# First feed-forward's gated result in separate tiles of high and low parts, and weights placed 64 bytes beyond the stream mod 256

## The chip, the cores and the metric

The kernel runs on one core of a Trainium2 chip. The metric is device time in microseconds of one execution. A profiled execution gives the trace from which the tables and rows below come; times between single matmuls are read from that.

## The reference

A decoder layer on 272 tokens (16 learned meta tokens ahead of 256) of width 2048: feed-forward, a mixer of differential attention beside a short gated convolution, and a second feed-forward. What bears on the change:

```python
def swiglu_ffn(h, w_gu, w_down):
    gate, up = jnp.split(h @ w_gu, 2, axis=-1)
    return (jax.nn.silu(gate) * up) @ w_down

h = rms_norm(s, norm_ffn1[layer])
s = s + 0.5 * swiglu_ffn(h, ffn1_w_gu[layer], ffn1_w_down[layer])
h = rms_norm(s, norm_mix[layer])
q, k, v, b_gate, c_gate, u = jnp.split(h @ w_in[layer], splits, axis=-1)
...
v = c_gate * u          # short convolution over time, then b_gate * y
```

Everything is float32; the feed-forward's inner width is 5632.

## The kernel before

**Numbers in two parts.** Every matmul operand is split into a high part (a copy as fp32r) and a low part (value minus high part). A product is three matmuls: weights high by activations high, weights high by activations low, weights low by activations high (lines 329 to 331 in `linear`). ScalarE casts the weights from the load buffer `st` into `wh` (line 313), VectorE subtracts into `wl` (line 318).

**A linear.** `linear` computes four 128-wide column groups at once, each in a PSUM bank, over all chunks of 128 contraction rows. Per chunk it issues 4 x 3 matmuls of 128x128 weights by n columns of activations: n = 272 for gate, up, down, k and v, and n = 258 for c and u, which start at token 14 (`n0 = NMETA - 2`). For n up to 256 the high and low parts go through in one matmul of 2n columns. Weights of two chunks share a buffer of `wh` and one of `wl` (three buffers each, from `wpool`); a load (SyncE's queue, 1 MB) brings four chunks into one of four buffers.

**Stages.** The first feed-forward runs in two halves of 6 and 5 groups of 512 inner columns. In each half, `gate_up` runs for each group a linear for gate (`pg`) and one for up (`pu`) over 16 chunks of `h1`, and puts the gated product into `m`; then four down linears (`pd`) run over the half's 24 or 20 chunks of `m`, and add to the stream `s`. After it come k, q, b, v, with attention steps between matmuls, then c and u, the gates and branch projections (`g`, `z`), `w_out` (`o`), and the second feed-forward, which is written with other functions and uses `linear` no more.

**Where operands lie.** A word is 4 bytes. An `Act` tile holds two chunks, each with its high and its low part, one after the other. For `h1` and `h2` a part is 320 words long (1280 bytes) and its 272 tokens begin at word 48, so every part is read from 192 bytes mod 256 of the tile's start. For `m` a part is 272 words (1088 bytes = 4 x 256 + 64), so the four parts of a tile begin at 0 (high, even chunk), 64 (low, even), 128 (high, odd) and 192 (low, odd) mod 256. Weights of a column group begin at a multiple of 512 bytes in `wh` and `wl`. All buffers of `act`, `big`, `wh` and `wl` have sizes that are multiples of 256 bytes, and in the built program all of them start at the same residue mod 256.

**Order.** The order on each engine follows the order of the code, with evictions and small steps put in by chunk number (`EVICT_AT`, `side_at`, `later_at`); a tile's buffer is free when its last reader is done.

Of the kernel before, what the change touches and what calls it, by code (L numbers as in the profile page):

```python
# [9 lines left out]
F32 = mybir.dt.float32  # L10
F32R = mybir.dt.float32r
# [4 lines left out]
P = 128  # L16
D = 2048
SEQ = 256
NMETA = 16
# [3 lines left out]
GC = 4  # L23
GW = GC * P
W2 = D // 2
NH = 8
HD = 64
# [29 lines left out]
def decoder_layer(ctx: ExitStack, tc: tile.TileContext, t, out):  # L57
    nc = tc.nc

    const = ctx.enter_context(tc.tile_pool(name="const", bufs=1))  # L60
    wpool = ctx.enter_context(tc.tile_pool(name="w", bufs=W_BUFS))
    apool = ctx.enter_context(tc.tile_pool(name="a", bufs=N_ACT))
    aux = ctx.enter_context(tc.tile_pool(name="aux", bufs=N_AUX))
    tmp = ctx.enter_context(tc.tile_pool(name="tmp", bufs=2))
    psum = ctx.enter_context(tc.tile_pool(name="ps", bufs=8, space=bass.MemoryType.PSUM))

    def bank(name):
        return psum.tile([P, 512], F32, tag="acc", name=name)

    def wide(shape, name):  # L70
        return tmp.tile(shape, F32, tag="wide", bufs=4, name=name)
# [37 lines left out]
    vrows = const.tile([NV, P], F32, name="vrows")  # L109
    G_MIX, G_FFN2, G_CONV, G_SUB = 0, DC, 2 * DC, NV - 1  # L110

    lamv = const.tile([P, 4, HD], F32, name="lamv")

    def load_vectors():
        for g0, src in ((G_MIX, t["norm_mix"][0]), (G_FFN2, t["norm_ffn2"][0])):
# [11 lines left out]
        out=mask[:, T - P :],  # L127
        in_=mask[:, T - P :],
# [41 lines left out]
    class Act:  # L170


        def __init__(self, name, chunks, width, wide_slots=(), piece=None):
            self.width, self.lead = width, 0 if piece is None else piece - width
            self.tiles = []
            for g in range(chunks // 2):
                if g in wide_slots:
                    w = piece or width
                    raw = apool.tile([P, 4 * PIECE], F32R, tag="big", bufs=N_BIG, name=f"{name}{g}")
                    self.tiles.append(raw[:, : 4 * w].rearrange("p (c l w) -> p c l w", c=2, l=2))  # L180
                else:
                    self.tiles.append(apool.tile([P, 2, 2, width], F32R, tag="act", name=f"{name}{g}"))
# [3 lines left out]

        def part(self, c, lo, t0, t1):
            return self.tiles[c // 2][:, c % 2, lo, self.lead + t0 : self.lead + t1]

    def split(act, g, src):  # L190

        for k in range(2):
            tl, f = act.tiles[2 * g + k], src[:, 2 * k : 2 * k + 2, :]
            nc.scalar.copy(out=tl[:, :, 0, :], in_=f)
            nc.vector.tensor_sub(tl[:, :, 1, :], f, tl[:, :, 0, :].bitcast(F32))
# [73 lines left out]
    def drain():  # L269
        while ahead:  # L270
            ahead.pop(0)[0]()

    def linear(act, chunks, w, k0, c0, t0, t1, name, evict, before=None, side_at=(5, 9, 13), after=None, later_at=LATER_AT):

        n = t1 - t0
        kb = KB
        nl = LB * kb
        starts = list(range(0, len(chunks), kb))  # L280
        if before is not None:
            starts.insert(1, 1)
        acc = [bank(f"{name}_{j}") for j in range(GC)]
        ready = {}
        for b, b1 in zip(starts, starts[1:] + [len(chunks)]):
            blk = chunks[b:b1]
            r0 = (k0 + blk[0]) * P
            wh = wpool.tile([P, kb, GW], F32R, tag="wh", name="wh")
            wl = wpool.tile([P, kb, GW], F32R, tag="wl", name="wl")
            m = len(blk)  # L290
            if before is not None or b % nl == 0:
                st = wpool.tile([P, LB * kb, GW], F32, tag="st", bufs=ST_BUFS, name="st")
                ml = m if before is not None else min(nl, len(chunks) - b)
                with ExitStack() as order:
                    for ins in x_load:
                        order.enter_context(tc.issue_after(ins))
                    x_load.clear()
                    last_load[:] = [
                        nc.sync.dma_start(
                            out=st[:, :ml, :],  # L300
                            in_=w[r0 : r0 + ml * P, c0 : c0 + GW].rearrange("(c p) f -> p c f", p=P),
                        ).ins
                    ]
            sw = st[:, :m, :] if before is not None else st[:, b % nl : b % nl + m, :]
            with ExitStack() as order:
                if before is not None and b == 0:
                    with tc.issue_after(nc.scalar.copy(out=wh[:, :m, :], in_=sw).ins):
                        ready[0] = before(blk)
                if before is not None:
                    for ins in ready.pop(b):  # L310
                        order.enter_context(tc.issue_after(ins))
                if before is None or b:
                    nc.scalar.copy(out=wh[:, :m, :], in_=sw)  # L313
                if before is None and b:
                    for ins in ahead_of_split:
                        order.enter_context(tc.issue_after(ins))
                    ahead_of_split.clear()
                nc.vector.tensor_sub(wl[:, :m, :], sw, wh[:, :m, :].bitcast(F32))  # L318
            if before is not None and b1 < len(chunks):
                ready[b1] = before(chunks[b1 : starts[starts.index(b1) + 1] if b1 < starts[-1] else None])  # L320
            drain()
            for i, c in enumerate(blk):
                first, last = b + i == 0, b + i == len(chunks) - 1
                for j in range(GC):
                    a, f = acc[j][:, :n], slice(j * P, (j + 1) * P)
                    if 2 * n <= 512:
                        nc.tensor.matmul(acc[j][:, : 2 * n], wh[:, i, f], act.both(c, t0, t1), start=first, stop=False)  # L327
                    else:
                        nc.tensor.matmul(a, wh[:, i, f], act.part(c, 0, t0, t1), start=first, stop=False)  # L329
                        nc.tensor.matmul(a, wh[:, i, f], act.part(c, 1, t0, t1), start=False, stop=False)  # L330
                    nc.tensor.matmul(a, wl[:, i, f], act.part(c, 0, t0, t1), start=False, stop=last)  # L331
                if b + i == EVICT_AT:
                    flush()
                if b + i in later_at and later:
                    later.pop(0)()
                if b + i in side_at and side:
                    side.pop(0)()
                if after is not None:
                    after(b + i)
        flush()  # L340
        pending.append(lambda: evict(acc))

    def flush():
        while pending:
            pending.pop(0)()
# [92 lines left out]
    def gate_up(h, half, w_gu, norm, n0, before=None):  # L438

        n = T - n0  # L440
        m = Act("m", len(half) * GC, n)
        for gi, g in enumerate(half):
            sg = wide([P, GC, T], "sg")

            def gate(pg, sg=sg):
                rstd = norm.rstd[:, n0:]
                for j in range(GC):
                    gt = tmp.tile([P, T], F32, tag="gt", name="gt")
                    nc.vector.tensor_mul(gt[:, :n], pg[j][:, :n], rstd)
                    nc.scalar.activation(gt[:, :n], gt[:, :n], AF.Silu)  # L450
                    nc.vector.tensor_mul(sg[:, j, :n], gt[:, :n], rstd)

            def up(pu, sg=sg, gi=gi):
                for j in range(GC):
                    nc.vector.tensor_mul(sg[:, j, :n], pu[j][:, :n], sg[:, j, :n])
                split(m, gi, sg[:, :, :n])

            linear(h, list(range(DC)), w_gu, 0, g * GW, 0, n, "pg", gate, before=before)
            before = None
            linear(h, list(range(DC)), w_gu, 0, F + g * GW, 0, n, "pu", up)  # L460
        return m
# [274 lines left out]
    for half in halves:  # L736
        m = gate_up(h1, half, t["ffn1_w_gu"][0], norm1, 0, before1 if half is halves[0] else None)
# [370 lines left out]
    for half in thirds:  # L1108
        m = Act("m", len(half) * GC, SEQ, range(4))
# [3 lines left out]
        if final:  # L1113
            for q in range(2):
                nc.gpsimd.dma_start(
                    out=gfin[q],
                    in_=t["norm_final"][q * W2 : (q + 1) * W2].rearrange("(o d) -> o d", o=1).to_broadcast([P, W2]),
                )
        ma = Mixed(m, 0, True)
        for u in range(2):  # L1120
# [23 lines left out]
            chunks = list(range(len(half) * GC))  # L1144
# [41 lines left out]
```

## Time and profile before

| | |
|---|---|
| median of 3 runs | 2161.79 us (2161.72 to 2163.14) |
| profiled execution, its own time | 2161.81 us |
| its span, first to last instruction | 2160.0 us |
| TensorE, busy share of the span | 99% |
| VectorE, ScalarE, GpSimd | 73%, 51%, 4% |
| granted TensorE clock, mean | 0.999 |
| DMA engines in the first 700 us | about half busy |

A row of a group gives line, engine, operation, output <- inputs, shape and count, then busy time, mean ns of one, and the idle time before them with what ended it. Matmuls overlap, and their ends are modelled, so their durations add up to more than the time they fill; the time from start to start is what they cost. A row of the windows view gives a stretch of the span, its length, busy time and count of the chosen instructions on each engine, the granted clock, the DMA engines' share and GB/s. PEld is the load of weights into the array, PE the matmul itself.

### The profile page before, as it was taken

What the parts mean: (1) busy time and instruction counts of PE and PEld (TensorE: products, weight loads), DVE (VectorE), ACT (ScalarE), POOL (GpSimd) and SP (SyncE); (2) the same over time, 40 slices, a digit from 0 to 9 for tenths busy, and PEclk for the clock granted to TensorE, in tenths of its full rate; (3) what the DMA queues carried; (4) which work ended last, traced back from release to release, by engine and by line L of the source; (5) the groups of instructions that cost most, each with busy time, mean ns of one, the idle gap of its engine ahead of it and who ended that gap; (6) DMA issues with size and microseconds to landing.
All of it is one profiled execution on the core that took longest, in us unless ns stands there. A gap on an engine that the chain in (4) does not pass through costs nothing.

```text
span 2160.0 us, 33235 instructions
## 1 busy us (share of the span) xinstructions
PE 2147.3 (99%) x13349; PEld 1943.6 (90%) x13349; DVE 1566.5 (73%) x2054; ACT 1091.2 (51%) x1379; POOL 82.8 (4%) x93
## 2 busy tenths in 40 slices
PE   9999999999999999999999999999999999999998
PEld 9999999999999998899998888888888888888886
DVE  8555554445555567866887778678999899988997
ACT  6443343334433444545445555456665566655664
POOL 0000000000000000000000000001100111012100
PEclk9999999999999999999999999999999999999999
DMA  7555555555555555544456556557886989679954
GB/s 256 176 178 180 181 181 174 175 179 181 176 176 176 176 176 191 180 158 136 156 187 203 194 197 222 193 189 237 273 259 198 289 283 281 226 224 312 280 198 156
DMA packets 205216, 440.76 MB, mean 204 GB/s; under 512 B 10557, under 2 KB 11270, under 8 KB 205062
## 3 DMA queue, kind: packets, MB, share of 16 engines
q1 hardware_dynamic: 188118, 398.13, 53.9%
q0 software_dynamic: 16480, 39.85, 8.3%
q8 instruction: 104, 1.70, 0.3%
q10 hardware_dynamic: 464, 0.66, 0.1%
q14 instruction: 50, 0.41, 0.1%
HBM read 431.26 MB, written 2.10 MB: 201 GB/s over the span
## 4 chain that ended last, share of the span: by engine, by line
PE 97%; DMA 1%; DVE 1%; ACT 0%; issue 0%; POOL 0%; SPq 0%; DVEq 0%; ACTq 0%
PE pg L522 6%; PE pg L524 6%; PE pg L523 6%; PE pd L331 4%; PE pd L329 4%; PE pd L330 4%; PE pu L329 4%; PE pu L331 4%; PE pu L330 4%; PE pg L331 4%; PE pg L329 4%; PE pg L330 4%; PE o L327 3%; PE pd L524 3%; PE pd L523 3%; PE pd L522 3%
## 5 line engine op out<-in xcount | busy, mean ns | idle before, releaser
L318 DVE TENSOR_TENSOR wl<-st,wh 128x1024 fp32r<-128x1024 f32 (+1 forms) x361 | 439.9, 1220 | 399.5 <-ACT wh L313 399.1
L313 ACT CAST wh<-st 128x1024 fp32r<-128x1024 f32 (+1 forms) x360 | 376.6, 1047 | 529.8 <-PE pu L330 151.1
L432 DVE TENSOR_TENSOR wl<-st,wh 128x1024 fp32r<-128x1024 f32 (+1 forms) x392 | 437.2, 1122 | 68.6 <-ACT wh L431 66.7
L431 ACT CAST wh<-st 128x1024 fp32r<-128x1024 f32 (+1 forms) x392 | 371.6, 973 | 216.2 <-PE pdx L523 45.1
L431 ACT CAST wh<-t 128x1024 fp32r<-128x1024 f32 x142 | 148.2, 1052 | 206.2 <-DVE t L562 135.3
L432 DVE TENSOR_TENSOR wl<-t,wh 128x1024 fp32r<-128x1024 f32 x142 | 172.3, 1222 | 57.6 <-ACT wh L431 52.7
L329 PE MATMUL pd<-m,wh 128*128 128x272 f32 x704 | 203.0, 288 | 0.0
L331 PE MATMUL pd<-m,wl 128*128 128x272 f32 x704 | 203.0, 288 | 0.0
L330 PE MATMUL pd<-m,wh 128*128 128x272 f32 x704 | 202.4, 288 | 0.0
L329 PE MATMUL pu<-h,wh 128*128 128x272 f32 x704 | 201.9, 287 | 0.0
L331 PE MATMUL pu<-h,wl 128*128 128x272 f32 x704 | 201.7, 287 | 0.0
L330 PE MATMUL pu<-h,wh 128*128 128x272 f32 x704 | 201.7, 287 | 0.0
L329 PE MATMUL pg<-h,wh 128*128 128x272 f32 x704 | 201.6, 287 | 0.0
L330 PE MATMUL pg<-h,wh 128*128 128x272 f32 x704 | 201.2, 287 | 0.1
L331 PE MATMUL pg<-h,wl 128*128 128x272 f32 x704 | 199.6, 287 | 0.1
L524 PE MATMUL pg<-wl,h 128*128 128x512 f32 x399 | 156.2, 391 | 0.0
L523 PE MATMUL pg<-wh,h 128*128 128x512 f32 x399 | 156.2, 391 | 0.0
L522 PE MATMUL pg<-wh,h 128*128 128x512 f32 x399 | 155.5, 390 | 0.0
L330 PEld LDWEIGHTS pg<-h,wh 128*128 128x128 f32 x704 | 132.6, 188 | 0.4 <-DVE h L202 0.4
L329 PEld LDWEIGHTS pg<-h,wh 128*128 128x128 f32 x704 | 132.6, 188 | 0.4 <-ACT h L201 0.2
L330 PEld LDWEIGHTS pd<-m,wh 128*128 128x128 f32 x704 | 132.7, 189 | 0.0
L330 PEld LDWEIGHTS pu<-h,wh 128*128 128x128 f32 x704 | 132.6, 188 | 0.0
(369 smaller groups left out, 4847.7 us busy)
## 6 DMA issues: line engine op xcount, KB each, us to landing
st<-in_ffn_w_gu_dram SPq DMA_DIRECT2D x183, 512.0 KB, 6.1
st<-in_ffn_w_down_dram SPq DMA_DIRECT2D x88, 1024.0 KB, 5.1
st<-in_ffn_w_gu_dram SPq DMA_DIRECT2D x84, 1024.0 KB, 4.9
st<-in_w_in_dram SPq DMA_DIRECT2D x48, 1024.0 KB, 5.2
st<-in_w_gate_dram SPq DMA_DIRECT2D x64, 512.0 KB, 4.3
t<-in_ffn_w_gu_dram POOLq DMA_DIRECT2D x64, 512.0 KB, 7.3
st<-in_w_branch_dram SPq DMA_DIRECT2D x32, 512.0 KB, 4.9
st<-in_w_out_dram SPq DMA_DIRECT2D x16, 1024.0 KB, 5.0
```

The costliest lines, as they stand in the source:

```text
L313: nc.scalar.copy(out=wh[:, :m, :], in_=sw)
L318: nc.vector.tensor_sub(wl[:, :m, :], sw, wh[:, :m, :].bitcast(F32))
L327: nc.tensor.matmul(acc[j][:, : 2 * n], wh[:, i, f], act.both(c, t0, t1), start=first, stop=False)
L329: nc.tensor.matmul(a, wh[:, i, f], act.part(c, 0, t0, t1), start=first, stop=False)
L330: nc.tensor.matmul(a, wh[:, i, f], act.part(c, 1, t0, t1), start=False, stop=False)
L331: nc.tensor.matmul(a, wl[:, i, f], act.part(c, 0, t0, t1), start=False, stop=last)
L431: part_last[:] = [nc.scalar.copy(out=wh, in_=src).ins]
L432: part_last.append(nc.vector.tensor_sub(wl, src, wh.bitcast(F32)).ins)
L522: nc.tensor.matmul(ps[k], hi, wh, start=first, stop=False)
L523: nc.tensor.matmul(ps[k], lo, wh, start=False, stop=False)
L524: nc.tensor.matmul(ps[k], hi, wl, start=False, stop=left[k] == 0)
```

## The change

`m` of the first feed-forward becomes an `Apart`: for each group of four chunks one tile with the high parts and one with the low parts. A part is still 1088 bytes, so chunk c of either tile begins at 64 x (c mod 4) mod 256. For these linears the weights of the two chunks are put into a wider buffer, with a start and a step that put those of chunk c at 64 x (c mod 4 + 1) mod 256. For the other linears the weights start `t0` words into their buffer: 0 for all but c and u, 14 (56 bytes) for those, whose stream starts 14 words later too. Buffers of `wh` and `wl` thus grow from 4096 to 4352 bytes; to make room, `lamv` (1024 bytes, used once for the attention's lambda) takes a buffer of the tag `sc` in place of its own.

```diff
-    lamv = const.tile([P, 4, HD], F32, name="lamv")
+    lamv = tmp.tile([P, 4, HD], F32, tag="sc", name="lamv")
...
+    class Apart:
+        step = GW + NMETA
+
+        def __init__(self, name, chunks, width):
+            self.width = width
+            self.tiles = [
+                [apool.tile([P, GC, width], F32R, tag="act", name=f"{name}{lo}{g}") for lo in "hl"]
+                for g in range(chunks // GC)
+            ]
+
+        def part(self, c, lo, t0, t1):
+            return self.tiles[c // GC][lo][:, c % GC, t0:t1]
+
+        def weights(self, raw, c):
+            f = c % GC * NMETA
+            return raw[:, f : f + 2 * self.step].rearrange("p (c f) -> p c f", c=2)[:, :, NMETA:]
+
+        def split(self, g, src):
+            hi, lo = self.tiles[g]
+            for k in range(2):
+                cs = slice(2 * k, 2 * k + 2)
+                nc.scalar.copy(out=hi[:, cs, :], in_=src[:, cs, :])
+                nc.vector.tensor_sub(lo[:, cs, :], src[:, cs, :], hi[:, cs, :].bitcast(F32))
...
-            wh = wpool.tile([P, kb, GW], F32R, tag="wh", name="wh")
-            wl = wpool.tile([P, kb, GW], F32R, tag="wl", name="wl")
+            if isinstance(act, Apart):
+                wh, wl = (
+                    act.weights(wpool.tile([P, 2 * act.step + 2 * NMETA], F32R, tag=nm, name=nm), blk[0])
+                    for nm in ("wh", "wl")
+                )
+            else:
+                wh, wl = (
+                    wpool.tile([P, t0 + kb * GW], F32R, tag=nm, name=nm)[:, t0:].rearrange("p (c f) -> p c f", c=kb)
+                    for nm in ("wh", "wl")
+                )
...
-        m = Act("m", len(half) * GC, n)
+        m = Apart("m", len(half) * GC, n)
...
-                split(m, gi, sg[:, :, :n])
+                m.split(gi, sg[:, :, :n])
```

On TensorE, at the start of the first half's down linears, chunk 0 and column groups 0 and 1; before:

```order
L329 MATMUL pd_3316<-m_132,wh 128x272
L330 MATMUL pd_3316<-m_132,wh 128x272
L331 MATMUL pd_3316<-m_132,wl 128x272
L329 MATMUL pd_3317<-m_132,wh 128x272
L330 MATMUL pd_3317<-m_132,wh 128x272
L331 MATMUL pd_3317<-m_132,wl 128x272
```

and now:

```order
L363 MATMUL pd_3316<-mh_132,wh 128x272
L364 MATMUL pd_3316<-ml_133,wh 128x272
L365 MATMUL pd_3316<-mh_132,wl 128x272
L363 MATMUL pd_3317<-mh_132,wh 128x272
L364 MATMUL pd_3317<-ml_133,wh 128x272
L365 MATMUL pd_3317<-mh_132,wl 128x272
```

The order is the same; the low part comes from another tile. On VectorE, around the same place (the last eviction of up, then the first down linear's weights), before:

```order
L318 TENSOR_TENSOR wl<-st,wh 128x1024
L195 TENSOR_TENSOR m_142<-sg,m_142 128x2x272
L195 TENSOR_TENSOR m_143<-sg,m_143 128x2x272
L318 TENSOR_TENSOR wl<-st,wh 128x1024 x11
L747 SCALAR_TENSOR_TENSOR s_112<-pd_3316,s_112 128x272
```

and now:

```order
L352 TENSOR_TENSOR wl<-st,wh 128x2x512
L214 TENSOR_TENSOR ml_143<-sg,mh_142 128x544 x2
L352 TENSOR_TENSOR wl<-st,wh 128x2x512 x11
L781 SCALAR_TENSOR_TENSOR s_112<-pd_3316,s_112 128x272
```

Again nothing has moved. The weights' low parts are written as two runs of 512 with a gap, the low parts of `m` as one run of 544. On all five engines every instruction stands where it stood.

## The prediction

> **What bounds the kernel now.** I read the page first: the span, the busy shares and the chain of work that ended last.
>
> ```profile
> span 2160.0 us, 33235 instructions
> PE 2147.3 (99%) x13349; PEld 1943.6 (90%) x13349; DVE 1566.5 (73%) x2054; ACT 1091.2 (51%) x1379; POOL 82.8 (4%) x93
> PE 97%; DMA 1%; DVE 1%; ACT 0%; issue 0%; POOL 0%; SPq 0%; DVEq 0%; ACTq 0%
> ```
>
> TensorE sets the end: 97% of the chain is matmuls. Next the list of waits, on TensorE alone; the columns are total us, times, longest.
>
> ```profile
> PE pd L362 <- DVE wl L432: 1.7, 2, 1.2
> PE warm L82 <- DVE ones L76: 1.1, 1, 1.1
> PE pt L686 <- DMA xin<-in_x_dram: 0.3, 1, 0.3
> PE pd L360 <- ACT wh L431: 0.2, 1, 0.2
> PE c L331 <- DVE wl L318: 0.2, 1, 0.2
> ```
>
> All its waits together are 3.5 us, and none is in a down linear of the first feed-forward. So nothing can be gained there but by matmuls that follow each other faster. How fast they do is not in their durations, which the page's groups give (busy us, mean ns):
>
> ```profile
> L329 PE MATMUL pd<-m,wh 128*128 128x272 f32 x704 | 203.0, 288 | 0.0
> L329 PE MATMUL pu<-h,wh 128*128 128x272 f32 x704 | 201.9, 287 | 0.0
> ```
>
> These overlap (1152 of them at 288 ns would take 332 us, and a window below shows them in 145). What counts is the time from one start to the next, and the windows give that, since each of the following is filled by one kind of matmul. The columns are from:to and length, then TensorE's busy time and count, granted clock, DMA share, GB/s. First four linears of gate and up (tile pu, and tile pg for the last of them), then the down linears of both halves (tile pd).
>
> ```profile
> 83.80:107.48 23.68, 23.68 (x192) 1.00 0.53 178
> 131.16:154.84 23.68, 23.68 (x192) 1.00 0.52 178
> 465.24:488.92 23.68, 23.68 (x192) 1.00 0.51 178
> 441.56:465.24 23.68, 23.68 (x192) 1.00 0.52 179
> ...
> 296.92:441.56 144.64, 144.64 (x1152) 1.00 0.52 175
> 678.36:799.28 120.92, 120.79 (x960) 1.00 0.51 175
> ```
>
> Gate and up: 23.68 / 192 = 123.33 ns a matmul, the same in each of the four. Down: 144.64 / 1152 = 125.56 ns, 2.22 ns more, with the same shape (128x128 weights, 272 columns), the same order of three products, the same clock and the same DMA load. The second down window holds another matmul in its middle:
>
> ```profile
> 687.27 0.29 PE L331 MATMUL pd<-m,wl 128*128 128x272 f32 x1
> 687.49 0.27 PE L150 MATMUL vp<-ident,vrows 57*128 57x57 f32 x1
> 687.68 0.39 PE L329 MATMUL pd<-m,wh 128*128 128x272 f32 x1
> ```
>
> That hole is 0.41 us long where 0.125 would do, so 0.28 us of the 120.92 is not the down linear's: (120.92 - 0.28) / 960 = 125.67 ns. Both halves agree.
>
> What differs is where the operands lie. The timeline shows that they are read together:
>
> ```profile
> 320.02 0.29 PE L330 MATMUL pd<-m,wh 128*128 128x272 f32 x1
> 320.03 0.19 PEld L331 LDWEIGHTS pd<-m,wl 128*128 128x128 f32 x1
> 320.15 0.29 PE L331 MATMUL pd<-m,wl 128*128 128x272 f32 x1
> 320.15 0.19 PEld L329 LDWEIGHTS pd<-m,wh 128*128 128x128 f32 x1
> ```
>
> The load of the next weights starts within 0.01 us of the matmul that streams its 272 columns. For gate, up, k and v the tile width of 320 and the lead of 48 words put the stream at 192 bytes mod 256 of its tile, the weights at 0, so the weights lie 64 beyond it. In the down linears a part is 1088 bytes = 4 x 256 + 64: the four parts of a tile of m stand at 0, 64, 128 and 192, and the weights at 0. Weights thus lie 0, 192, 128 or 64 beyond; 64 only for the low part of odd chunks, one matmul in six.
>
> **The change part by part.** It removes no instruction and adds none. On all five engines the program has the same instructions in the same order, DMAs and their queues too; only addresses, tile names and the folding of some shapes differ. So there is no new wait by order, and the terms are rates.
>
> *Down linears.* With the tiles apart, chunk c of the high or the low tile stands at 64 c mod 256, and the weights, moved by 64 (c + 1), are 64 beyond in all 2112 matmuls. If the distance is what makes 125.6 of 123.33, the first half saves 144.64 - 1152 x 0.12333 = 2.56 us and the second 120.64 - 960 x 0.12333 = 2.24 us: 4.8 us. This price is seen: in the four linears above, of two kinds and from both halves, which read other buffers. Bounds: 0, if the distance isn't the cause, and 4.8, since no 272-column matmul here goes faster than gate and up. I take 4.8.
>
> [...]
>
> *c and u.* They stream from word 14, 56 bytes on, so the stream is at 248 mod 256 of its tile; the weights were at 0, 8 beyond, and are now at 56, 64 beyond. Undisturbed stretches of 258 columns (tile c, tile u), and one of 512 (tile g):
>
> ```profile
> 996.32:1002.04 5.72, 5.72 (x48) 1.00 0.48 174
> 1079.80:1085.52 5.72, 5.72 (x48) 1.00 0.54 186
> ...
> 1195.58:1202.38 6.80, 6.80 (x30) 1.00 0.47 162
> ```
>
> That is 5.72 / 48 = 119.2 ns. From 512 columns (6.80 / 30 = 226.7) to 272 (123.33) a column is worth 0.43 ns, so 258 columns at gate's rate would take 123.33 - 14 x 0.43 = 117.3 ns. There are 768 such matmuls (2 groups, c and u, 16 chunks, 4 x 3): at most 1.9 x 768 = 1.4 us. What the trace does not show is the 64 bytes at a start that is no multiple of 32 bytes; the weights' own reads get such a start now too. Lower bound: the largest excess over gate's rate seen here, 2.3 ns on each, a loss of 1.8 us. The cause is the same as in the down linears, so I lean to the upper end and take 1.0 us.
>
> *What has to keep pace.* In the first half's down linears (windows, all engines: TensorE, weight loads, VectorE, ScalarE, GpSimd; then VectorE's and ScalarE's groups in that window), and in c and u:
>
> ```profile
> 296.90:441.50 144.60, 144.60 (x1154) 144.60 (x1153) 65.66 (x67) 51.53 (x50) 0.00 (x0) 1.00 0.52 175
> 996.30:1104.40 108.10, 107.78 (x892) 104.10 (x891) 82.41 (x164) 53.42 (x108) 0.00 (x0) 1.00 0.46 156
> ...
> L318 DVE TENSOR_TENSOR wl<-st,wh 128x1024 fp32r<-128x1024 f32 x48 | 58.8, 1225 | 78.9 <-ACT wh L313 78.9
> L313 ACT CAST wh<-st 128x1024 fp32r<-128x1024 f32 x48 | 50.4, 1051 | 93.1 <-PE pd L330 85.3 <-DVE s L747 5.8 <-PE pu L330 1.9
> ```
>
> Weights of two chunks need 1.05 us of ScalarE and 1.23 of VectorE, and TensorE takes 24 x 0.123 = 2.96 us for them, with three buffers each. VectorE is idle 78.9 us waiting for the cast, 1.6 us per split. The split now writes two runs of 512 with a gap. No row has that form; from -0.1 to +0.3 us an instruction covers the spread of the forms shown (1.05 to 1.23 for 1024 elements), and all of it is hidden here at the cost of nothing. With no cover it would be 88 splits x 0.3 = 26 us, but for that they would have to become 1.6 us longer. Four casts and subtractions per group of m keep their count, and write whole runs. In c and u VectorE is busy 82 of 108 us; the one wait there is 0.2 us, and I take 0.1 us off the gain for it. The DMA moves 175 GB/s there and 178 under gate's rate, so it follows.
>
> **Sum.** The profiled execution took 2161.81 us, 1.81 beyond its span, and the median of the runs is 2161.79, the same. 4.8 + 1.0 - 0.1 = 5.7 us off: 2161.8 - 5.7 = 2156.1 us. What a measurement tells from no change is about 0.2%, 4.3 us.
>
> **The rivals.** *Distance is not the cause*: stream and weight load leave each other alone, and the down linears are slower for another reason. Then both terms are 0, and the time is 2161.8 us. [...] For it: the 512-column rows of g have distance 0 and still stand at 226.7 in a steady beat. Against: w_out's linear, also at distance 0, which alternates 512 and 256 columns (tile o):
>
> ```profile
> 1371.75:1393.04 21.29, 21.29 (x120) 1.00 0.43 149
> 1428.12:1450.40 22.28, 22.28 (x128) 1.00 0.52 178
> ```
>
> It takes 174 to 177 ns a matmul, where 226.7 and 123.33 - 16 x 0.43 = 116.4 would give a mean of 171.6. And the down linears have no row that sets them apart but the addresses.
>
> *Only part of it.* Gate's stream always starts at one place mod 256, the new down stream at four. If the place counts as well as the distance, one chunk in four gets the gain: 4.8 / 4 = 1.2 us, and c and u nothing: 2160.6 us. Against it: 1088 bytes pass through all residues anyway, whatever the start.
>
> *Slower: the weight buffers' spacing.* A buffer of wh or wl grows from 4096 to 4352 bytes, so the weights of every linear shift against their stream by multiples of 256. If a period above 256 counts, the 4224 matmuls of gate and up and the 768 of k and v could fall to the down linears' old rate: 4992 x 2.2 ns = 11.0 us, 2156.1 + 11.0 = 2167.1 us; it loses from 5.7 / 4992 = 1.1 ns each. Against it: h's tiles are 5120 bytes apart and its parts 1280, so the distances above 256 differ from chunk to chunk already, and the rows of 23.68 do not move.
>
> *It doesn't do what it says*: ruled out as far as addresses go. All act, wh and wl tiles start at one residue mod 256 in the built program, and its 2112 and 768 matmuls all have the 64.
>
> **How the numbers follow.** Forecast (down at gate's rate, c and u somewhere between their bounds): 0.76, from 2161.8 - 4.8 - 1.4 = 2155.6 to 2161.8 - 4.8 + 1.8 = 2158.8. No effect 0.12, a part 0.06, slower 0.06. The range, 2154.3 to 2160.8, takes in the forecast with about 1.3 us of spread between executions (the runs lie 1.4 apart) and the partial case, and leaves out no effect and slower, 0.18. Faster by over 4.3 us, under 2157.5: the forecast unless c and u lose more than 0.5 us, 0.68. Within: the rest of the forecast, no effect, a part, 0.26. Slower: 0.06.
>
> **What would show it.** The windows of pd: 1152 matmuls in about 142.1 us and 960 in about 118.7 (with the hole of 0.28), in the place of 144.64 and 120.92; windows of gate and up again at 23.68. A stretch of 48 matmuls of c or u in 5.63 to 5.68 us; over 5.72 says that the unaligned start costs. VectorE's splits stay under 1.6 us and TensorE's list of waits without a row of pd L331's kind in the first feed-forward. The prediction is wrong if pd stays near 125.5 ns, or if a linear of pg or pu leaves 23.68.

## The result: 3.2 us less, and the profile after

| | before | after |
|---|---|---|
| median of 20 runs each | 2162.14 us (2161.67 to 2166.18) | 2158.93 us (2158.32 to 2161.79) |
| ratio of the times, 95% interval | | 0.9985 (0.9978 to 0.9992) |
| profiled execution, its own time | 2161.81 us | 2158.63 us |

The interval leaves out 1, so the change is a gain, but of 0.15%: less than the 0.2% that the prediction counted as the bound of "no change". The forecast was 5.7 us; 3.2 came. The outcome that the prediction held most likely, faster by over 4.3 us (0.68), did not come. The head of the page of the changed kernel, with the chain's share by engine:

```profile
span 2156.9 us, 33235 instructions
PE 2143.5 (99%) x13349; PEld 1940.6 (90%) x13349; DVE 1566.8 (73%) x2054; ACT 1091.5 (51%) x1379; POOL 82.8 (4%) x93
PE 97%; DMA 1%; DVE 1%; ACT 0%; issue 0%; POOL 0%; SPq 0%; DVEq 0%; ACTq 0%
```

The same instructions, the same bound: TensorE is 3.8 us less busy, the other engines as before. TensorE's waits (total us, times, longest):

```profile
PE pd L396 <- DVE wl L466: 1.7, 2, 1.2
PE warm L82 <- DVE ones L76: 1.1, 1, 1.1
PE pg L363 <- ACT h L227: 0.9, 1, 0.9
...
PE pd L394 <- ACT wh L465: 0.3, 1, 0.3
PE c L365 <- DVE wl L352: 0.2, 1, 0.2
```

No wait has come into a down linear of the first feed-forward (L363 to L365 with pd). The one for h, 0.9 us, is new and lies in the first gate linear, which ends 0.13 us earlier all the same (36.11 us for 36.24). So the difference must be in how closely matmuls follow each other, and the windows of the changed kernel show where (from:to, length, TensorE's busy time and count, clock, DMA share, GB/s): the two halves' down linears (tile pd), two linears of up (pu), a stretch of c and one of u, and the whole stage from the start of c to the end of u.

```profile
296.80:439.68 142.88, 142.88 (x1152) 1.00 0.54 177
676.48:795.97 119.49, 119.36 (x960) 1.00 0.54 177
...
83.68:107.36 23.68, 23.68 (x192) 1.00 0.52 178
463.36:487.04 23.68, 23.68 (x192) 1.00 0.51 178
...
993.00:998.77 5.77, 5.77 (x48) 1.00 0.47 175
...
1076.81:1082.57 5.76, 5.76 (x48) 1.00 0.55 185
...
993.00:1101.59 108.59, 108.38 (x893) 1.00 0.47 155
```

and that last stage in the kernel before:

```profile
996.32:1104.48 108.16, 107.83 (x893) 1.00 0.46 156
```

The down linears gained 144.64 - 142.88 = 1.76 us and 120.92 - 119.49 = 1.43 us, 3.19 together: 142.88 / 1152 = 124.03 ns a matmul in place of 125.56, where 123.33 was expected. Gate and up did not move. c and u, expected to gain 1.0 us, lost: 5.77 / 48 = 120.2 ns in place of 119.2, and their stage is 108.59 - 108.16 = 0.43 us longer. 3.19 - 0.43 = 2.76 of the 3.18 us between the two profiled executions; the rest, 0.4, is in stages whose distances the change leaves alone (0.3 of it in that of g and z), and such amounts come and go between executions (below).

Where in a chunk the down linears lose the rest is seen from the starts of the 12 matmuls (four column groups by three products) of a chunk. Mean ns from each start to the next, over 95 chunks of the first half, worked out from the trace; the last number of a row is the sum:

```
position     1      2      3      4      5      6      7      8      9     10     11     12    sum
before   125.5  125.8  126.1  125.3  123.9  125.5  126.9  126.0  124.5  125.4  124.7  127.1  1506.7
after    125.7  120.0  125.0  126.7  122.6  124.1  122.6  124.1  122.6  124.1  122.6  128.3  1488.3
```

After the change a chunk's middle (positions 5 to 11) runs at gate's rate (122.6 and 124.1 in turn, mean 123.35), and only the change of chunk, with the first matmuls behind it, costs more: 1488.3 - 12 x 123.33 = 8.3 ns. 176 chunks of two halves make 1.46 us of it. That is where most of the missing 1.6 us is. Beside the last matmul of a chunk the first weights of the next are loaded: in the changed kernel's trace that load starts 3 to 4 ns after the matmul, at each of the first half's 95 edges. The change puts the weights of chunk c 64 bytes beyond the stream of chunk c; those of chunk c + 1 are 64 further, so in this one load they lie 128 beyond the stream that runs.

### The profile page after: what moved, and what is told of

Read it like the earlier page. It is cut to its first block, busy times and chain, and to the rows that moved or that the text cites. A ratio compares the mean times of both kernels' runs of the same rounds, so it can differ in the third digit from the quotient of the medians.

```text
span 2156.9 us, 33235 instructions
## 1 busy us (share of the span) xinstructions
PE 2143.5 (99%) x13349; PEld 1940.6 (90%) x13349; DVE 1566.8 (73%) x2054; ACT 1091.5 (51%) x1379; POOL 82.8 (4%) x93
## 4 chain that ended last, share of the span: by engine, by line
PE 97%; DMA 1%; DVE 1%; ACT 0%; issue 0%; POOL 0%; SPq 0%; DVEq 0%; ACTq 0%
PE pg L556 6%; PE pg L557 6%; PE pg L558 6%; PE pd L365 4%; PE pd L363 4%; PE pu L364 4%; PE pu L365 4%; PE pu L363 4%; PE pd L364 4%; PE pg L365 4%; PE pg L364 4%; PE pg L363 4%; PE o L361 3%; PE pd L557 3%; PE pd L558 3%; PE pd L556 3%
## 5 line engine op out<-in xcount | busy, mean ns | idle before, releaser
L365 PE MATMUL pd<-mh,wl 128*128 128x272 f32 x704 | 203.1, 288 | 0.0
L363 PE MATMUL pg<-h,wh 128*128 128x272 f32 x704 | 201.6, 287 | 0.9 <-ACT h L227 0.9
L363 PE MATMUL pd<-mh,wh 128*128 128x272 f32 x704 | 202.3, 287 | 0.0
L363 PE MATMUL pu<-h,wh 128*128 128x272 f32 x704 | 201.9, 287 | 0.0
L365 PE MATMUL pu<-h,wl 128*128 128x272 f32 x704 | 201.7, 287 | 0.0
L364 PE MATMUL pd<-ml,wh 128*128 128x272 f32 x704 | 200.7, 285 | 0.0
L365 PE MATMUL pg<-h,wl 128*128 128x272 f32 x704 | 199.6, 287 | 0.1
L363 PEld LDWEIGHTS pg<-h,wh 128*128 128x128 f32 x704 | 132.6, 188 | 1.5 <-ACT h L227 1.1
L364 PEld LDWEIGHTS pd<-ml,wh 128*128 128x128 f32 x704 | 133.5, 190 | 0.0
L363 PEld LDWEIGHTS pu<-h,wh 128*128 128x128 f32 x704 | 132.6, 188 | 0.0
```

## The experiments

All are edits of the changed kernel. A number called a distance is how many bytes the start of the weights that are loaded lies beyond the start of the stream, mod 256; that whole multiples of 256 are left out fits gate and up, which stayed at 23.68 us when the weight buffers grew from 4096 to 4352 bytes. Each run's time is set beside runs of the kernel before on the same chip.

**1. Distance alone, in gate and up.** Only the weights' start in their buffer differs from group to group, with the same shape, order and stream; the stream's high and low parts lie in one tile here. This is the test of the prediction's main claim.

```diff
+SCAN = (0, 8, 16, 24, 32, 40, 48, 56, 4, 12, 60)
+SCAN_CU = (6, 22, 30, 46)
...
+                w0 = t0 if woff is None else woff
...
-                    wpool.tile([P, t0 + kb * GW], F32R, tag=nm, name=nm)[:, t0:].rearrange("p (c f) -> p c f", c=kb)
+                    wpool.tile([P, w0 + kb * GW], F32R, tag=nm, name=nm)[:, w0:].rearrange("p (c f) -> p c f", c=kb)
...
+            linear(h, list(range(DC)), w_gu, 0, F + g * GW, 0, n, "pu", up, woff=SCAN[g])
```

> The changed kernel, with the weights of gate and up put at another place for each of the 11 groups: 64, 96, 128, 160, 192, 224, 0, 32, 80, 112, 48 bytes beyond the stream mod 256; the four linears of c and u at 32, 96, 128, 192. Theory (what counts is the distance from a matmul's stream to the weights loaded beside it): a full linear of gate or up stays at 23.68 us (123.33 ns a matmul) at 64, and goes to 124.5 to 126.5 ns at 0, 128 and 192; c and u differ among themselves by 1 to 3 ns. Rival (distance means nothing, the down linears are slower for another reason): all eleven groups at 23.68.

Measured: 2170.74 us once (before: 2162.11). The up linears (tile pu) of six groups, with distances 96, 128, 224, 0, 32 and 80:

```profile
83.89:107.57 23.68, 23.68 (x192) 1.00 0.55 178
131.89:156.21 24.32, 24.32 (x192) 1.00 0.53 173
...
277.62:301.76 24.14, 24.14 (x192) 1.00 0.51 176
...
468.69:492.76 24.07, 24.07 (x192) 1.00 0.52 175
516.82:540.89 24.07, 24.07 (x192) 1.00 0.55 176
565.20:589.52 24.32, 24.32 (x192) 1.00 0.52 173
```

96 is as good as 64 (23.68); 0 and 32 cost 2.0 ns a matmul more (24.07 / 192 = 125.4), 224 costs 2.4, 128 costs 3.3 (126.7), and 160 and 192 stood at 24.32 and 24.31. Distances 80, 112 and 48 also cost 24.32, though 80 lies between the two best; there the weights begin 16, 48 and 240 bytes into their buffer, and in the other eight groups at a multiple of 32, so this price can't be put down to the distance alone (in experiment 5, 268 columns at a distance of 48 with the weights at 0 took 23.68). So where the weights lie is a cause by itself, and its price is 2 to 3.3 ns for 272 columns. The writing of the weights moved with them, but it doesn't explain the price: the matmuls during which no weights were cast or subtracted took 123.2 ns at 96, 125.2 at 0 and 126.2 at 128 (33, 37 and 40 of the 192, from the trace). That it is the distance to the stream, and not the place of the weights, this run alone can't tell, since its stream stands in one place. The down linears of the changed kernel can: there streams and weights stand at four places in step, and a chunk takes 1488.3 or 1488.4 ns at each of the four. In c and u distances of 32, 96 and 192 ran at 119.8 to 120 ns, no better than 64. The linear of c with 128 did something else (tile c; the columns as above):

```profile
1062.68:1070.50 7.82, 7.45 (x54) 1.00 0.41 133
1080.07:1088.67 8.60, 8.60 (x72) 1.00 0.41 130
```

The undisturbed 72 took 8.60 / 72 = 119.4 ns; the 54 before them 7.45 / 54 = 138 ns, at the full clock; no run here tells why.

**2. c and u as they were.** The weights of c and u go back to the start of their buffer, 8 bytes beyond the stream; the down linears keep the change.

```diff
-                    wpool.tile([P, t0 + kb * GW], F32R, tag=nm, name=nm)[:, t0:].rearrange("p (c f) -> p c f", c=kb)
+                    wpool.tile([P, kb * GW], F32R, tag=nm, name=nm).rearrange("p (c f) -> p c f", c=kb)
```

> The changed kernel with c's and u's weights at word 0 of their buffer again, as in the kernel before (8 bytes beyond the stream). Theory (it is the shift that made c and u slower, by about 0.8 ns on 768 matmuls): c and u back at 119.2 ns, 0.6 to 0.7 us less than the changed kernel, about 2158.3. Rival (c and u are slower for the buffers' new spacing or by the order of other work): no change against 2158.9.

Measured: 2159.44 us (2158.62 to 2160.78), 0.9988 of before (0.9978 to 0.9997). A stretch of c, one of u and the first half's down linears:

```profile
993.35:999.08 5.73, 5.73 (x48) 1.00 0.48 176
...
1076.82:1082.54 5.72, 5.72 (x48) 1.00 0.59 186
...
297.17:440.04 142.87, 142.87 (x1152) 1.00 0.53 177
```

c and u are back at 119.2 ns, and their stage, 108.14 us, is 0.45 us shorter in the trace than with the change: the shift of c and u alone costs that. The median does not show it; one wait in the last down linear of the second feed-forward, which no edit here touches, took 1.2 us in this execution and 0.3 in the changed kernel's.

**3. The edge of a chunk at 64.** In the down linears column group 0's low weights get a place of their own, 64 bytes before the rest, and its products are ordered so that they are read first: the load beside the last matmul of a chunk then lies 64, not 128, beyond the stream.

```diff
+                rh, rl = (wpool.tile([P, 2 * act.step + 2 * NMETA], F32R, tag=nm, name=nm) for nm in ("wh", "wl"))
+                wh, wl = act.weights(rh, blk[0]), act.weights(rl, blk[0])
+                f0 = blk[0] % GC * NMETA
+                wl0 = rl[:, f0 : f0 + 2 * act.step].rearrange("p (c f) -> p c f", c=2)[:, :, :P]
...
-                nc.vector.tensor_sub(wl[:, :m, :], sw, wh[:, :m, :].bitcast(F32))
+                if isinstance(act, Apart):
+                    nc.vector.tensor_sub(wl0[:, :m, :], sw[:, :, :P], wh[:, :m, :P].bitcast(F32))
+                    nc.vector.tensor_sub(wl[:, :m, P:], sw[:, :, P:], wh[:, :m, P:].bitcast(F32))
...
+                    if j == 0 and isinstance(act, Apart):
+                        nc.tensor.matmul(a, wl0[:, i, :], act.part(c, 0, t0, t1), start=first, stop=False)
+                        nc.tensor.matmul(a, wh[:, i, f], act.part(c, 0, t0, t1), start=False, stop=False)
+                        nc.tensor.matmul(a, wh[:, i, f], act.part(c, 1, t0, t1), start=False, stop=last)
+                        continue
```

> The changed kernel with one matmul's weights moved at each change of chunk in the down linears: column group 0 starts with low weights by high part, and these 128 low weights lie 64 bytes lower, so that the weights loaded beside the last matmul of the chunk before are 64 beyond its stream too, and not 128. Two subtractions of 256 and 768 in the place of one of 1024. Theory (the loss against gate and up is the edge between chunks, 8 ns each, 176 of them): pd at 123.3 ns, windows of 142.1 and 118.7 us, 1.4 us less than the changed kernel, about 2157.5. Rival (high and low parts in two tiles cost something in every chunk): pd stays at 124.0 ns, 2158.9 or a little more.

Measured: 2159.75 us (2157.75 to 2160.61), 0.9989 of before (0.998 to 0.9998). The first half, and in the second the 888 matmuls behind the small transpose (vp) that interrupts it:

```profile
296.85:439.09 142.24, 142.24 (x1152) 1.00 0.53 178
685.07:794.82 109.75, 109.75 (x888) 1.00 0.53 177
```

142.24 / 1152 = 123.47 ns, and by position a chunk takes 1481.7 ns: 1.7 over gate's rate where it was 8.3. So the edge is where the rest went, and it goes when the load that reaches into the next chunk is given the good distance (the edit also turns the order of group 0's products, which wasn't tried alone). It also shows which weights count: the first matmul of each chunk now has its own weights 0 beyond its stream, the next one's 64, and the whole chunk is within those 1.7 ns. The rival, that reading high and low from two tiles costs the rest, is out, since both tiles are still read. VectorE's extra instruction per split is hidden (groups of the first half's window; busy us, mean ns, idle before and its releaser):

```profile
L354 DVE TENSOR_TENSOR wl<-st,wh 128x768 fp32r<-128x768 f32 x46 | 43.8, 951 | 0.0
L353 DVE TENSOR_TENSOR wl<-st,wh 128x256 fp32r<-128x256 f32 x46 | 19.5, 425 | 70.0 <-ACT wh L347 70.0
```

It still waits 70.0 us there. Yet the median did not fall below the changed kernel's, and the profiled execution took 2158.56 us where the changed kernel's took 2158.63. The trace has the gain (k starts 1.15 us earlier) and where most of it goes, in this kernel's waits of TensorE:

```profile
PE pd L405 <- DVE wl L475: 1.7, 2, 1.2
PE warm L82 <- DVE ones L76: 1.1, 1, 1.1
PE pd L403 <- ACT wh L474: 1.1, 1, 1.1
```

The third stood at 0.3 us in the changed kernel. Over the traced executions here it took 0.2 to 2.2 us, so totals that are 1 us apart are not told apart; the rate inside a stage is. Seven of this kernel's eleven executions took 2159.6 us or more; what they lost stands in no trace.

**4. The same scan with 512 columns.** The weights of gate and up in the second feed-forward, which stream 512 columns, are moved by the same amounts from group to group. In this stage the two operands have changed roles: the weights are the stream, and the activations are what is loaded. Moving the weights 32 bytes on thus leaves the load 32 bytes before the stream's start, 224 beyond it mod 256.

```diff
+        mix_off[0] = SCAN[g]
...
-            else (held_tile(nm) if held else wpool.tile([P, 2, GW], F32R, tag=nm, name=nm))
+            else (
+                held_tile(nm) if held
+                else wpool.tile([P, 2 * GW + 64], F32R, tag=nm, name=nm)[:, mix_off[0] : mix_off[0] + 2 * GW].rearrange(
+                    "p (q f) -> p q f", q=2
+                )
+            )
```

> The changed kernel with the second feed-forward's gate and up weights, which there are the 512-column stream, moved by 0, 32, 64, 96, 128, 160, 192, 224, 16, 48, 240 bytes in their buffers, one for each group; the activations loaded beside them stay, at distance 0 before. [...] Rival (with 512 columns the load has time enough): 226.7 in every group.

Measured: 2168.9 us once (before: 2162.11). Stretches from one start to the thirtieth after it, TensorE alone (the count takes in the matmul at the edge), with weights moved by 0, 32, 64 and 192 bytes, that is with distances of 0, 224, 192 and 64:

```profile
1480.97:1487.77 6.80, 6.80 (x31) 1.00 1.01 274
1513.53:1520.52 6.99, 6.99 (x31) 1.00 0.91 299
1556.09:1563.02 6.93, 6.93 (x31) 1.00 0.94 299
...
1805.78:1812.78 7.00, 7.00 (x31) 1.00 0.52 169
```

6.80 / 30 = 226.7 ns at distance 0, as before; 233.0, 231.0 and 233.3 at 224, 192 and 64, and 230 to 234 at all others. None was under 226.7. Distance counts here as well, but the one it has, 0, is the best, and 64 is not. So "64 beyond" is no rule by itself.

**5. What makes a distance good: the length.** In gate and up of the first feed-forward the first 8, 4 or 14 of the 272 tokens are left out in some groups, and their gated result is set to 0, so this kernel computes less: 264, 268 or 258 columns, each with some distances. One theory had the good place 64 to 96 bytes beyond the stream's start whatever its length; the other had it where the stream ends, or 32 behind that (272 columns are 1088 bytes, 64 mod 256; 264 are 1056, 32; 258 are 1032, 8; 512 are 2048, 0).

```diff
+SCAN = ((0, 0), (8, 0), (8, 8), (8, 16), (8, 24), (8, 56), (4, 0), (4, 8), (14, 0), (14, 8), (14, 14))
...
+            a0, woff = SCAN[g]
+            na = T - a0
+            if a0:
+                nc.vector.memset(sg[:, :, :a0], 0.0)
...
-            linear(h, list(range(DC)), w_gu, 0, F + g * GW, 0, n, "pu", up)
+            linear(h, list(range(DC)), w_gu, 0, F + g * GW, a0, T, "pu", up, woff=woff)
```

> The changed kernel with shorter streams in gate and up of the first feed-forward: groups 1 to 5 leave out the first 8 tokens (264 columns), groups 6 and 7 the first 4 (268), groups 8 to 10 the first 14 (258); the gated result of the tokens left out is set to zero, so the work on these meta tokens is left out. The streams still end at the same place, 224 mod 256; weights lie at word 0, 8, 16, 24, 56 for groups 1 to 5, at 0, 8 for groups 6, 7 and at 0, 8, 14 for groups 8 to 10. c and u: weights at words 8, 16, 56, 24, that is 40, 72, 232, 104 beyond; w_out: 0, 64, 32, 192 beyond. [...] Group 10 is the changed kernel's own shift, expected 120.

Measured: 2151.36 us. The up linears: five of 264 columns with distances 32, 64, 96, 128 and 0, one of 268 (48), three of 258 (8, 40 and 64):

```profile
83.53:106.57 23.04, 23.04 (x192) 1.00 0.55 183
129.64:152.69 23.05, 23.05 (x192) 1.00 0.55 183
176.05:199.40 23.35, 23.35 (x192) 1.00 0.56 181
223.08:246.77 23.69, 23.69 (x192) 1.00 0.53 178
269.81:292.84 23.03, 23.03 (x192) 1.00 0.55 185
...
459.39:483.07 23.68, 23.68 (x192) 1.00 0.53 178
...
553.29:576.15 22.86, 22.86 (x192) 1.00 0.56 184
599.19:622.23 23.04, 23.04 (x192) 1.00 0.56 183
645.26:668.30 23.04, 23.04 (x192) 1.00 0.54 183
```

With 264 columns 32 is good and 96 is not, so the first theory falls. The second has the first four right and misses the fifth: 0, which is 32 before the stream's end, is as good. c and u had distances of 40, 72, 232 and 104 in this kernel. 40, which is 32 behind the stream's end, took 120.0 ns, 72 took 119.9 and 104 took 121.0; the best was c at 232, again 32 before the stream's end (48 steps from start to start; the count takes in the edges):

```profile
1062.63:1068.33 5.70, 5.70 (x50) 1.00 0.56 190
```

That is 5.70 / 48 = 118.8 ns. The runs thus say "about where the stream ends", for 258, 264, 272 and 512 columns; the exact rule stays open. The rows also bear on the price of a column. 272 and 264 columns take 123.33 (23.68 / 192) and 120.0 ns, 0.42 ns a column apart; but 268 take 123.33 too, and 258 take 120.0 with two of the distances. So the price does not go by the column alone. The streams also start at different places in h's tile: 192 mod 256 for 272 columns, 224 for 264, 208 for 268 and 248 for 258. 264, 268 and 258 columns were tried from one start each, so no run parts the length from the start. At their good distances 258 columns go lower: 118.8 ns at 232, and 22.86 / 192 = 119.06 ns at 8, which is how c and u stood before the change. In w_out's linear the four distances tried told nothing that could be separated from its other unevenness.

**6. Experiments 2 and 3 together.** c and u back, and the edge at 64; the diffs are those two.

> The changed kernel with the edge of the chunks mended as in e3_edge and c's and u's weights at word 0 as in e2_cu_back. Theory (the edge costs 1.2 to 1.4 us, the shift of c and u 0.4 to 0.7, independent of each other): pd at 123.5 ns, c and u at 119.2, together 1.6 to 2.0 us under the changed kernel of the same call, and c's end 1.6 us earlier in the trace. Rival (what is gained there is waited for at the end): c ends earlier, the time is that of the changed kernel.

Measured: 2159.31 us (2157.85 to 2160.84), 0.9985 of before (0.9977 to 0.9994). The down linears, as in experiment 3:

```profile
297.08:439.32 142.24, 142.24 (x1152) 1.00 0.52 178
685.30:796.77 111.47, 111.47 (x888) 1.00 0.51 175
```

The first half is right, the second is not: 111.47 / 888 = 125.5 ns behind the transpose, where experiment 3 had 109.75 / 888 = 123.6 from the same addresses in these linears. Nothing in the second half differs from experiment 3.

**7. The changed kernel again.** It ran beside 6, to set that against it on one chip.

> The changed kernel once more, beside e6_both on one chip: about 2158.9 us, pd at 124.0 ns, c and u at 120.0. Both theories: the same as its first runs within 1 us; it is the yardstick for e6_both.

Measured: 2159.6 us (2158.59 to 2160.62), 0.9989 of before (0.998 to 0.9998). Behind the transpose:

```profile
685.99:796.24 110.25, 110.25 (x888) 1.00 0.52 176
```

110.25 / 888 = 124.2 ns. Experiment 6 lost 1.2 us to it here, and gained 0.6 in the first half and 0.4 in c and u; the medians are alike.

**8. The chunks of a pair in reverse.** The second chunk of each pair goes first, with c and u back. The load across an edge then lies 0 beyond the stream, not 128.

```diff
-            for i, c in enumerate(blk):
-                first, last = b + i == 0, b + i == len(chunks) - 1
+            turn = isinstance(act, Apart)
+            for k, (i, c) in enumerate(reversed(list(enumerate(blk))) if turn else enumerate(blk)):
+                first, last = b + k == 0, b + k == len(chunks) - 1
```

> The changed kernel with c's and u's weights at word 0, and in the down linears the second chunk of each pair taken before the first. At every edge between chunks the next weights then lie at 0 beyond the stream in the place of 128; the other 1936 pairs of a stream and the load beside it stay at 64. Theory (the edge costs by its distance; as a steady state 0 cost 2.0 ns a matmul over gate's rate in e1_scan, 128 cost 3.3): edges of about 5 ns in the place of 8.3, pd at 123.7 to 123.8 ns, c ends 0.9 us earlier than in the changed kernel (0.5 from the edges, 0.4 from c and u). Rival (an edge costs because the place changes, whatever the distance): pd at 124.0.

Measured: 2159.21 us (2158.24 to 2159.98), 0.9986 of before (0.9977 to 0.9995).

```profile
296.92:439.80 142.88, 142.88 (x1152) 1.00 0.53 177
```

Not a hundredth less than with the change: 8.3 ns an edge again in the mean, spread otherwise over the positions (126.2, 126.3, 121.2, ... 125.4; the chunks take 1485.0 and 1491.7 ns in turn). My sizing of an edge by the steady price of its distance (2.0 against 3.3 ns) was wrong. At the two distances off the good place that were tried, 0 and 128, an edge costs the same in the mean, and at 64 it costs 1.7.

**9 and 10. The slow second half.** Kernel 6 was run again as it was; and then with the first of the small steps inside the first of a half's four down linears, which in the second half is the transpose, put one chunk later.

> e6_both once more. There the second half's down linears ran at 125.5 ns a matmul, with the addresses of the first half, which ran at 123.5, and of e3_edge, where both halves ran at 123.5. Theory (the order of streams and loads has more than one steady beat at the same addresses, and an interruption can throw it from one to the other): 123.5 in both halves this time, or again 125.5, and then again from the interruption by the transpose of the vectors on. Rival (something in that kernel makes the second half slow): 125.5 from that place on, as before.

Measured: 2161.88 us once (before: 2162.14). Behind the transpose:

```profile
685.25:796.72 111.47, 111.47 (x888) 1.00 0.52 175
```

It came again, on another chip, to the hundredth; what followed it was the wait in the last down linear, 2.2 us here. The other kernel:

```diff
-            linear(m, list(range(len(half) * GC)), t["ffn1_w_down"][0], half[0] * GC, c * P, 0, T, "pd", down)
+            linear(
+                m, list(range(len(half) * GC)), t["ffn1_w_down"][0], half[0] * GC, c * P, 0, T, "pd", down,
+                side_at=(5, 9, 13) if c else (6, 9, 13),
+            )
```

> e6_both with the one small matmul that interrupts the second half's first down linear (the transpose of the vectors) one chunk later, after chunk 6 in the place of chunk 5; every address and all else as there. Theory (a second, slower beat exists at the same addresses, and where the interruption falls decides whether the linears after it are thrown into it): the second half can run at 123.5 ns as in e3_edge, and then c's end comes 1.6 us earlier than in the changed kernel and the time is 1 to 1.6 us under it. Rival (something else in that kernel slows the second half): 125.5 ns after the interruption, wherever it is.

Measured: 2158.18 us (2157.47 to 2159.26), 0.998 of before (0.9971 to 0.9989).

```profile
296.77:439.01 142.24, 142.24 (x1152) 1.00 0.54 178
686.47:794.74 108.27, 108.27 (x876) 1.00 0.52 176
```

108.27 / 876 = 123.6 ns: with the addresses unchanged and the interruption one chunk later, the rest of the half kept the faster rate, so nothing in those addresses forces the slower. That the chunk decides is not shown: experiment 3 was interrupted at the same chunk as 6, its down linears have the same addresses, and it kept 123.6. By the starts in the traces, the matmul behind the transpose began 199 and 198 ns after it in 3 and 10, and 196 ns after it in 6 and 9; whether so small a shift is the cause or only goes with the rate, four executions don't tell. Its median is the lowest of all kernels here that compute the whole layer, 4.1 us under before on the same chip. Against the changed kernel (2158.93 and 2159.6, beside other runs of the kernel before) the intervals overlap, so it is the likeliest best, not a proven one.

## Why the prediction was right, and where it was off

The measured time lies in the range, but with some luck: both terms of the sum gave less than forecast, and the total, 2158.9, lies just past the forecast's own band of 2155.6 to 2158.8. The range took it in because it was widened for the spread between executions and for the rival of a part.

**Distance is the cause: right.** Experiment 1 moves the weights alone and goes from 23.68 to 24.07 and 24.32 us, and the down linears, where weights and streams move in step, run alike at four places (1488.3 or 1488.4 ns a chunk). Why the distance counts, no run here shows.

**Down linears, 4.8 us: mis-sized.** They gave 3.19. The failing step is "the weights, moved by 64 (c + 1), are 64 beyond in all 2112 matmuls". That is so for a matmul and its own weights; but what counts for a stream is the load of the *next* weights, as the prediction's own timeline suggests and experiment 3 shows, and for one load in twelve the next weights belong to the next chunk. 176 such edges at 8.3 ns are 1.46 us; 0.15 of the shortfall is left without a place. With the edge at 64, experiment 3 came to 142.24 us for the first half, 0.16 from the 142.08 of gate's rate. The row that would have warned did not exist: gate's stream does not move from chunk to chunk, so it has no such edge.

**c and u, 1.0 us: wrong in sign.** They lost 0.4, within the term's bounds (-1.8 to 1.4) but not at the end that was chosen. Two steps failed. The 117.3 ns for 258 columns at gate's rate took 0.43 ns a column from two rows; experiment 5 has 258 columns at 118.8 ns at the best of its six distances, so the 119.2 of before was already within 0.4 ns of that. And "The cause is the same as in the down linears" took 64 as the good distance of any stream; c and u stood 8 beyond, which is where their 1032 bytes end, and the shift took them from there. The prediction named the sign that would show it ("over 5.72 says that the unaligned start costs"), and 5.77 came, but its reading was wrong: in experiment 5 weights that start 32 or 64 bytes into their buffer (multiples of 32, as 56 is not), 40 or 72 beyond the stream, take 120.0 and 119.9 as well. What was lost is the good place.

**What has to keep pace: right.** The split with two runs took 1226 ns where one run took 1225, as this group of the changed kernel in the first half's down window shows, and VectorE still waits 77.2 us for the casts:

```profile
L352 DVE TENSOR_TENSOR wl<-st,wh 128x1024 fp32r<-128x1024 f32 x48 | 58.9, 1226 | 77.2 <-ACT wh L347 77.2
```

The 0.1 us taken off for a tighter c and u was not needed; the wait there is 0.2 us as before.

**Rivals.** That distance is not the cause: refuted by experiment 1 (24.07 to 24.32 us in place of 23.68). That the place counts as well: the four places of the new stream run alike (1488.3 or 1488.4 ns a chunk in all of them), so no. That the buffers' spacing slows gate and up: 23.68, unmoved. The total fell between the forecast and "only part of it" by a mechanism none of the rivals had.

**Still open.** What sets which of two rates a stretch keeps behind an interruption (experiments 3, 6, 9, 10) is not known; why the good place for 264 columns is three starts wide was not tried further; and what makes 268 columns as slow as 272 (123.33 ns both), the length or where the stream starts, was not shown.

## What to carry to other kernels

Where TensorE is the bound and its matmuls overlap, read the time from start to start (here 123 to 127 ns for 272 columns, where the durations say 288), and look at the addresses of the stream together with the weights that are loaded *beside* it, which here were the next matmul's: pair each instruction with its neighbour, across loop edges too (8.3 ns a chunk here). A good distance found for one shape may belong to that shape alone (64 for 272 columns, 232 or 8 for 258, 0 for 512 here); scan it in one run, group by group, before it is carried over, since a scan costs one kernel and c and u would have been left alone. And a price per column taken from two rows holds no further than those rows; here 268 columns took 123.33 ns as 272 did, and where the stream starts may be part of it.

## What the runs showed of the hardware

All of these are times from start to start in the traces of the kernels above.

- The time of an fp32r matmul with 128x128 weights went with where the next weights lie mod 256 (experiment 1): for 272 columns 123.3 ns (64, 96 bytes beyond the stream), 125.4 (0, 32), 125.7 (224), 126.7 (128, 160, 192, and 48, 80, 112, where the weights began 240, 16 and 48 bytes into their buffer).
- The good place moved with the stream's length (experiment 5): for 264 columns 120.0 ns (0, 32, 64), 121.6 (96), 123.4 (128); for 258 columns 118.8 (232), 119.1 (8), 119.9 to 120.0 (40, 64, 72), 121.0 (104).
- The time did not go by the column alone (experiment 5): 123.33 ns for 272 and, at 48 beyond, for 268, whose stream starts at 208 mod 256; 120.0 for 264 and, at 40 and 64 beyond, for 258, whose stream starts at 248.
- For 512 columns the good place of the eleven tried was 0 (experiment 4): 226.7 ns against 230 to 234.
- The same addresses ran at two rates, 123.6 ns (experiments 3 and 10) and 125.5 (6 and 9), for the rest of a half behind a small matmul that interrupts; and 54 matmuls of 258 columns took 138 ns each once, at a granted clock of 1.00 (experiment 1).
